# Retention's normalization in a hybrid encoder layer: squares, their sums and the gate on other buffers, the gate's silu by tanh

## The chip, the cores and the metric

The kernel runs on one core of a Trainium2 chip. A core has TensorE (matmuls; it writes to PSUM, eight banks of 128 x 512 f32), VectorE, ScalarE (functions such as exp from a table that is loaded), GpSimd, and SyncE, whose queue issues most DMAs. In the profile they are PE (with PEld for weight loads), DVE, ACT, POOL and SP. The metric is the device time of one execution in microseconds, lower is better.

## The reference

One layer on x of 1024 tokens by 1024 features, in float32:

```python
u = x @ w_in                                  # split into rq, rk, rv, rg, aq, ak, av
y_ret = retention(rq, rk, rv)                 # 8 heads of 64, both directions, chunks of 128
y_ret = groupnorm(y_ret) * gn_gain * silu(rg)
y_att = windowed_gqa(aq, ak, av, sink)        # 8 query heads, window 128, ALiBi
h = layer_norm(alpha * x + concat(y_ret, y_att) @ w_out)
f = (silu(h @ w_gate) * (h @ w_up)) @ w_down + sigmoid(h @ w_pg) * (p @ w_pe)
out = layer_norm(alpha * h + f)
```

The group norm is over the 64 values of one head and token: subtract the mean, divide by sqrt(var + 1e-5). The change concerns this norm and the factor silu(rg).

## The kernel before

**Numbers.** Large products are made of three matmuls each: every operand is split into a high part (ScalarE, L71 or L580) and the rest (VectorE, L72 or L581). The value projection is centred per head beforehand (L359 to L362), so the retention's output has mean zero and the variance is a mean of squares.

**Stages.** First the projections of the first pair of heads, then a stage that works through four pairs of heads (retention and attention), then the output projection with the first layer norm, then the feed-forward part. The change lies in the second stage; that stage and the projection behind it together are about a third of the time.

**The stage of the four pairs.** Its lines give TensorE's order by hand: a list of steps in which `F` stands for a share of the queue of projection steps (`take`, L279). A step of that queue is three matmuls of 128 x 512, eight steps make one half (512 tokens) of a projection tile, into a bank "mm"; the queue holds the values, then the keys, queries and attention queries of pairs 1 to 3, at last the gates of pairs 0 to 3 (L718). So the first three gates run beside pair 3, and the fourth in the last list (L763). ScalarE, VectorE, GpSimd and SyncE are ordered by the program's planner in this stage. Each engine executes in its order.

**PSUM.** Four names of two banks each: "mm" (projections), "s" (scores), "t" (transposes and small products) and "o" (outputs). A bank is given in turn and has to be read out before TensorE writes it again.

**Retention, for one pair and one half `hh` of 512 tokens.** `out` (Y) sums 32 small matmuls into a bank "o", squares it on ScalarE into the buffer "sq" (L480) and copies it to `y` on VectorE (L481). `norm` (M) sums the squares of each head by matmuls against a 0/1 pattern, into a bank "t" (L487); VectorE scales the sums and adds epsilon (L490), GpSimd takes the power -0.5 (L491), and ScalarE spreads the factor to 512 columns in "rb" (L493). `turn` (X) transposes the factor into a bank "t" (L498), and VectorE multiplies `y` by it and the gain (L500). Buffers "sq" and "rb" exist once.

**What else uses "sq" and "t".** `decay_k` (L375) makes the decay matrix of the next pair in "sq" (ScalarE, then GpSimd). `gate` (L696) applies silu on ScalarE to the gate's bank "mm", into "sq" (L700), and VectorE multiplies `y` by it (L701). Attention of block n: `scores` (`sco`) with an exponential on ScalarE (L533), a scaling (L539), `turn` (`trn`) which transposes the probabilities into two banks "t" that ScalarE drains (L551, L553), and `values` (`val`) into a bank "o" (L563).

**Order around the change.** In a round of pairs 1 to 3, TensorE runs M(1) of the pair before near the start, X(1) some steps later, Y(0) in the middle, then M(0), the turn of block 5, the scores of block 7, Y(1), the values of blocks 4 and 5, X(0), and the turns of blocks 6 and 7 (L758 to L761). M(1) and X(1) of the last pair are in the last list.

**Beside it**, products of the output weights and of smaller weights are split and written to DRAM for later (`put`, L579): ScalarE, VectorE and a DMA, through one or two buffers.

Of the kernel before, what the change touches and what calls it, by code (L numbers as in the profile page):

```python
# [11 lines left out]
AF = mybir.ActivationFunctionType  # L12
ALU = mybir.AluOpType
# [3 lines left out]
P = 128  # L17
# [4 lines left out]
HF = 512  # L22
# [4 lines left out]
EPS = 1e-5  # L27
# [15 lines left out]
def layer(tc, xT, xn, w_first, w_mt, w_rv, w_out, w_pg, w_pe, pT, w_gu, w_dn,  # L43
          consts, dec_b, dec_c, sink, gng, lnp, out):
    nc = tc.nc
    act, dve, pool, pe, sp = nc.scalar, nc.vector, nc.gpsimd, nc.tensor, nc.sync
# [12 lines left out]
    def nm(s):  # L59
        uid[0] += 1  # L60
        return f"{s}{uid[0]}"

    def bank(tag, shape=(P, HF)):
        tag = ROLE[tag]
        return ps.tile(list(shape), F32, tag=tag, bufs=NB[tag], name=nm("b" + tag))
# [55 lines left out]
    def a_tile(shape, name, tag=None, dt=F32):  # L121

        turnA[0] += tag is None
        return big.tile(list(shape), dt, tag=tag or f"A{turnA[0] % 2}", bufs=4, name=nm(name))
# [8 lines left out]
    def bt(shape, tag, bufs=None, dt=F32):  # L133
        return bpool.tile(list(shape), dt, tag=tag, bufs=bufs, name=nm(tag))
# [15 lines left out]
    with tc.manual_schedule(engines={mybir.EngineType.DVE, mybir.EngineType.SP}):  # L150
        for kt in range(KT):
# [4 lines left out]
            if kt == 0:  # L156
                w0 = rawt(2 * HF)
                sp.dma_start(w0[:, :HF], w_first[0][:, :HF])
                for h in range(2):
                    sl = slice(h * HF, (h + 1) * HF)  # L160
# [18 lines left out]
            for h in range(2):  # L179
                sl = slice(h * HF, (h + 1) * HF)  # L180
                split(r[:, sl], xt[:, 0, sl], xt[:, 1, sl])
            xs.append(xt)
            for m, h in ([(m, h) for m in range(4) for h in range(2)] if kt else [(m, h) for h in range(2) for m in range(4)]):
                sl = slice(h * HF, (h + 1) * HF)
# [75 lines left out]
    for h in range(2):  # L260
        sl = slice(h * HF, (h + 1) * HF)
        b = st[1, h]
# [25 lines left out]
    def mtile(idx, evac):  # L288
        hold = {}

        def load():
            hold["w"] = unit2(w_mt[idx])

        def step(h, kt):
            if kt == 0:
                hold["b"] = bank("mm")
            b, w = hold["b"], hold["w"][kt // 4]
            c = slice((kt % 4) * P, (kt % 4 + 1) * P)
            sl = slice(h * HF, (h + 1) * HF)
            mm3(b, w[:, 0, c], w[:, 1, c], xs[kt][:, 0, sl], xs[kt][:, 1, sl], kt == 0, kt == KT - 1)  # L300
            if kt == KT - 1:
                evac(b, h)

        return [load], [lambda h=h, kt=kt: step(h, kt) for h in range(2) for kt in range(KT)]

    def enqueue(tiles):

        def both(f, g):
            f()
            g()  # L310

        for f in tiles[0][0]:
            f()
        for n, (_, steps) in enumerate(tiles):
            if n + 1 < len(tiles):
                for k, f in enumerate(tiles[n + 1][0]):
                    steps[2 * k] = lambda f=f, g=steps[2 * k]: both(f, g)
            queue.extend(steps)
# [63 lines left out]
    def state_tile():  # L382
        t = bt([P, 2, NT, 64], "states")
        pool.memset(t[0:64, :, 0, :], 0.0)
        pool.memset(t[64:128, :, NT - 1, :], 0.0)
        return t

    class Retention:
# [76 lines left out]
        def out(self, hh):  # L465

            o, pt, qq = bank("o", (P, 4, P)), self.pt[hh], self.qq[hh]
            for j in range(4):
                n = 4 * hh + j
                for part in range(2):  # L470
                    for h in range(2):
                        a = slice(64 * h, 64 * h + 64)
                        v = self.i * P + 64 * h
                        if part == 0:
                            pe.matmul(o[a, j, :], rv[:, n, v:v + 64], pt[:, h, j, :], start=True, stop=False)
                        else:
                            pe.matmul(o[a, j, :], self.states[:, h, n, :], qq[:, h, j, :], start=False, stop=True)
            of = o.rearrange("p n c -> p (n c)")
            sq = self.sq = bt([P, HF], "sq", 1)
            act.activation(sq, of, AF.Square)  # L480
            dve.tensor_copy(self.half(hh), of)  # L481

        def norm(self, hh):

            b = bank("t", (P, 4, 2))
            for j in range(4):
                pe.matmul(b[:, j, :], self.sq[:, j * P:(j + 1) * P], cst[:, C_BD:C_BD + 2], start=True, stop=True)  # L487
            sm = bt([P, 3, 8], "sm", 2)
            bf = b.rearrange("p n h -> p (n h)")
            dve.tensor_scalar(sm[:, 0, :], bf, 1.0 / 64, EPS, ALU.mult, ALU.add)  # L490
            pool.tensor_tensor(sm[:, 1, :], sm[:, 0, :], cst[:, C_MH:C_MH + 1].to_broadcast([P, 8]), ALU.pow)  # L491
            r = self.r[hh] = bt([P, 4, 2, 64], "rb")
            act.activation(r.rearrange("p n h e -> p (n h) e"), sm[:, 1, :].unsqueeze(2).to_broadcast([P, 8, 64]), AF.Copy)  # L493
# [172 lines left out]
    ys = [None] * 8  # L666

    def ytile(k):
        if ys[k] is None:
            ys[k] = a_tile([P, S], "y", "A0" if k < 4 else "A1")  # L670
        return ys[k]
# [24 lines left out]
    def gate(i):  # L696
        def f(b, h):
            s = bt([P, HF], "sq", 1)
            sl = slice(h * HF, (h + 1) * HF)
            act.activation(s, b, AF.Silu)  # L700
            dve.tensor_tensor(ys[2 * i][:, sl], ys[2 * i][:, sl], s, ALU.mult)  # L701
        return mtile(10 + i, f)

    def run(steps, total):
# [11 lines left out]
    F = None  # L716
    with tc.manual_schedule(engines={mybir.EngineType.PE}):
        enqueue([mtile(0, ev_av), proj_rv(), *project(1), *project(2), *project(3), gate(0), gate(1), gate(2), gate(3)])  # L718

        spare.append(bt([P, S], "aq", 3, F32R))  # L720
        twin = lambda t: t.rearrange("p (a b) -> p a b", a=2)
        ops = [twin(spare[1]), a_tile([P, 2, HF], "pro", "A0", F32R)]
        side.extend(presplit_out(0, ops, 17.5, 4))
        side.extend(presplit_out(1, ops, 44, 4, spare[:1]))
        a = Attention(0, ytile(1))
        sco, trn, val = (lambda n: (a.scores, n)), (lambda n: (a.turn, n)), (lambda n: (a.values, n))
        run([F, F, sco(0), F, sco(1), F], 16)
        run([F, (av_turn, 0), (av_turn, 1), F, trn(0), sco(2), F, trn(1), sco(3), F, val(0), val(1), trn(2), sco(4), F,
             trn(3), sco(5), F, val(2), val(3), trn(4), sco(6), F, trn(5), sco(7), F, val(4), val(5), trn(6), (decay_q, 0),
             F, trn(7), (decay_k, 0, 0), F, val(6), val(7), (decay_k, 0, 1), F], 64)  # L730
        assert not side and not later
        y0 = ytile(0)
        side.extend(presplit_gate())
        states = state_tile()
        r = Retention(0, y0, states)
        K, M = (lambda q: (r.keys, q)), (lambda q: (r.norm, q))
        Q, X = (lambda q: (r.scores, q)), (lambda q: (r.turn, q))
        Y = lambda hh: (r.out, hh)
        run([K(0), F, K(1), F, F, (r.kv,), Q(0), F, (r.scan,), F, F, F, Y(0), Q(1),
             F, M(0), (decay_q, 1), F, (decay_k, 1, 0), Y(1), X(0), (decay_k, 1, 1), F, F], 48)  # L740
        V = []
        for i in range(1, NPAIR):
            assert i == 1 or not side, len(side)
            M1, X1 = M(1), X(1)
            r = Retention(i, ytile(2 * i), states)
            a = Attention(i, ytile(2 * i + 1))
            if i == 2:
                late = [ytile(6), ytile(7)]
                op = twin(late[1].bitcast(F32R))
                side.extend(presplit_out(2, [op], 2, 3.5, late[:1]))  # L750
                side.extend(presplit_small(0, op, 30) + presplit_small(1, op, 38))
            elif i == 3:
                op = twin(bt([P, S], "aq", 3, F32R))
                side.extend(presplit_out(3, [op], 4, 3.5, [bt([P, S], "rk", 2)]))
                side.extend(presplit_small(2, op, 32) + presplit_small(3, op, 40))
            G = [(f, i + 1, *x) for f, x in ((decay_q, ()), (decay_k, (0,)), (decay_k, (1,)))] if i + 1 < NPAIR else \
                [(lambda: None,)] * 3
            run([*V, K(0), M1, F, K(1), sco(0), F, (r.kv,), Q(0), F, sco(1), X1, F, trn(0), sco(2), (r.scan,), F, trn(1),  # L758
                 sco(3), F, val(0), val(1), F, trn(2), sco(4), F, trn(3), sco(5), F,
                 Y(0), val(2), val(3), Q(1), F, G[0], trn(4), sco(6), M(0), F, G[1], trn(5), sco(7), F,  # L760
                 G[2], Y(1), val(4), val(5), X(0), F, trn(6), F, trn(7), F], 48)  # L761
            V = [val(6), val(7)]
        run([*V, M(1), F, X(1), F, F], 16)  # L763

# [34 lines left out]
    def four(k):  # L799
        return [bank(t) for t in sets[k]]  # L800
# [143 lines left out]
    X = four("a")  # L944
# [23 lines left out]
    X = four("a")  # L968
# [121 lines left out]
    X = four("a")  # L1090
# [43 lines left out]
    Y = four("a")  # L1134
# [162 lines left out]
    n = 0  # L1297
# [425 lines left out]
```

## Time and profile before

| what | us |
|---|---|
| median of three runs | 1194.67 (1194.57 to 1194.71) |
| the profiled execution | 1191.15 |
| its span, first to last instruction | 1189.4 |

The profile is of one execution. Its mean granted TensorE clock is 0.996 of full speed. In the table of stretches, between 200 and 260 us TensorE is busy 58.12 of 60.00, between 260 and 300 it is busy 38.18 of 40.00, between 300 and 340 it is busy 38.75 of 40.00, and between 340 and 375 it is busy 32.80 of 35.00; between 375 and 480 us it waits for nothing.

How to read the rows: in a timeline, the start in us, the duration, engine, line, operation, output <- input, shapes, count, and in brackets the engine's idle time just before and what ended it. In a group of instructions, after the bar the busy time and the mean in ns of one, after the second bar the idle time before them by what ended it. In a list of waits: who waited at which line, for whom, us in total, number of times, longest.

### The profile page before, as it was taken

The page shows a single profiled execution, that of the slowest core. Times are in us where ns is not written, and L with a number is a line of the kernel's source. Part 1 is how long each engine was busy: PE and PEld are TensorE (multiplying, and loading weights), DVE is VectorE, ACT ScalarE, POOL GpSimd, SP SyncE. Part 2 cuts the span into 40 slices and gives each one's busy share as a digit, 9 for nine tenths or more (in the row PEclk, how much of TensorE's full clock was granted, in tenths as well). Part 3 has the DMA queues.
Part 4 walks back from the last instruction along what each step waited for, and adds up shares of the span by engine and source line. Part 5 has one row for each costly group of instructions (what it writes and reads, how often), then busy time and mean ns, then how long its engine had stood idle before and what let it go on. Part 6 is the DMA issues. An engine that isn't in the chain of part 4 may idle for free.

```text
span 1189.4 us, 17057 instructions
## 1 busy us (share of the span) xinstructions
PE 1172.0 (99%) x6068; PEld 971.3 (82%) x6068; DVE 759.2 (64%) x1302; ACT 546.6 (46%) x1058; POOL 366.1 (31%) x346
## 2 busy tenths in 40 slices
PE   9999999999999999999999999999999999999997
PEld 7888888887787888888888888888888888888885
DVE  4566677675647788958754555545544566774677
ACT  5666348676876257114332333233333325562463
POOL 2001011202000022003756566564756342134242
PEclk9999999999999999999999999999999999999999
DMA  6346647445346854756223321333123169999977
GB/s 250 107 154 216 239 170 245 178 146 189 106 160 224 321 216 168 276 193 207 108 102 133 134 80 63 123 133 115 63 89 133 71 203 313 361 278 211 259 174 210
DMA packets 80661, 211.71 MB, mean 178 GB/s; under 512 B 9536, under 2 KB 14784, under 8 KB 80576
## 3 DMA queue, kind: packets, MB, share of 16 engines
q1 hardware_dynamic: 71936, 193.84, 45.9%
q0 software_dynamic: 8640, 16.78, 7.9%
q8 instruction: 48, 0.79, 0.3%
q14 instruction: 37, 0.30, 0.1%
HBM read 139.29 MB, written 62.13 MB: 169 GB/s over the span
## 4 chain that ended last, share of the span: by engine, by line
PE 75%; ACT 3%; DVE 2%; issue 1%; DMA 1%; POOL 0%; DVEq 0%; ACTq 0%; POOLq 0%
PE bs L782 6%; PE bs L781 6%; PE bs L780 6%; PE bt L780 6%; PE bt L781 6%; PE bt L782 6%; PE bmm L782 5%; PE bmm L781 5%; PE bmm L780 5%; PE bo L781 5%; PE bo L782 5%; PE bo L780 5%; PE bmm L77 2%; PE bmm L79 2%; PE bmm L78 1%; PE bo L563 1%
## 5 line engine op out<-in xcount | busy, mean ns | idle before, releaser
L77 PE MATMUL bmm<-H,w 128*128 128x512 f32 x240 | 98.2, 409 | 2.0 <-ACT sq L700 2.0
L79 PE MATMUL bmm<-H,w 128*128 128x512 f32 x240 | 94.9, 395 | 0.0
L78 PE MATMUL bmm<-H,w 128*128 128x512 f32 x240 | 94.5, 394 | 0.0
L1184 POOL TENSOR_TENSOR H<-ln 128x512 f32<-128x512 f32 x22 | 28.9, 1313 | 178.4 <-DMA ln<-in_w_gu 171.8
L1214 POOL TENSOR_TENSOR ev<-ev 128x512 f32<-128x512 f32 x33 | 54.6, 1656 | 91.5 <-DVE ev L1229 40.0
L72 DVE TENSOR_TENSOR w<-H,w 128x512 fp32r<-128x512 f32 x44 | 39.9, 908 | 62.7 <-ACT w L71 62.7
L72 DVE TENSOR_TENSOR w<-raw,w 128x512 fp32r<-128x512 f32 x56 | 44.9, 810 | 49.5 <-ACT w L71 49.3
L524 POOL COPY sc<-skb 128x1 f32<-128x1 f32 x64 | 14.6, 237 | 191.2 <-PE bt L551 167.2
L1212 ACT ACTIVATE ev<-ev 128x512 f32<-128x512 f32 x33 | 20.9, 633 | 103.0 <-DVE ev L1229 103.0
L1218 POOL TENSOR_TENSOR ev<-ev,ev 128x512 f32<-128x512 f32 x44 | 62.7, 1437 | 2.6
L72 DVE TENSOR_TENSOR u<-H,u 128x512 fp32r<-128x512 f32 x47 | 37.3, 793 | 38.4 <-ACT u L71 38.1
L77 PEld LDWEIGHTS bmm<-H,w 128*128 128x128 f32 x240 | 45.5, 190 | 11.9 <-ACT sq L700 2.1
L79 PEld LDWEIGHTS bmm<-H,w 128*128 128x128 f32 x240 | 45.4, 189 | 10.1
L78 PEld LDWEIGHTS bmm<-H,w 128*128 128x128 f32 x240 | 45.6, 190 | 7.9
L71 ACT ACTIVATE u<-H 128x512 fp32r<-128x512 f32 x47 | 29.6, 631 | 43.9 <-PE bt L782 9.0
L533 ACT ACTIVATE sc<-sc,st 128x385 f32<-128x385 f32 (+1 forms) x64 | 37.2, 585 | 18.9 <-DVE st L531 18.5
L529 DVE CUSTOM_DVE_ANT_0 sc<-cst,bs,skb 128x384 f32<-128x384 f32 (+1 forms) x64 | 34.9, 576 | 13.3 <-PE bs L528 8.1
L71 ACT ACTIVATE w<-raw 128x512 fp32r<-128x512 f32 x56 | 34.4, 624 | 15.6 <-PE bo L79 8.7
L891 POOL TENSOR_TENSOR stt<-stt,cst 128x1 f32<-128x1 f32 x8 | 12.2, 1520 | 86.0 <-DVE stt L890 86.0
L1188 POOL TENSOR_TENSOR H<-raw,H 128x512 f32<-128x512 f32 x22 | 37.8, 1717 | 0.0
L71 ACT ACTIVATE w<-H 128x512 fp32r<-128x512 f32 x44 | 27.4, 622 | 21.7 <-PE bt L782 6.3
L491 POOL TENSOR_TENSOR sm<-sm,cst 128x8 f32<-128x8 f32 x8 | 14.3, 1793 | 74.4 <-DVE sm L490 68.5
(811 smaller groups left out, 3778.2 us busy)
## 6 DMA issues: line engine op xcount, KB each, us to landing
ad<-ev SPq DMA_DIRECT2D x33, 512.0 KB, 2.6
pgd<-pro SPq DMA_DIRECT2D x28, 512.0 KB, 2.9
raw<-in_w_gu SPq DMA_DIRECT2D x22, 512.0 KB, 4.4
ln<-in_w_gu SPq DMA_DIRECT2D x22, 512.0 KB, 3.5
raw<-ad SPq DMA_DIRECT2D x40, 256.0 KB, 5.9
ln<-ad SPq DMA_DIRECT2D x37, 256.0 KB, 6.3
H<-in_w_dn SPq DMA_DIRECT2D x33, 256.0 KB, 6.9
wod<-aq SPq DMA_DIRECT2D x15, 512.0 KB, 2.7
```

The costliest lines, as they stand in the source:

```text
L71: act.activation(hi, raw, AF.Copy)
L72: dve.tensor_tensor(lo, raw, hi.bitcast(F32), ALU.subtract)
L77: pe.matmul(o, lh, rh, start=start, stop=False)
L78: pe.matmul(o, lh, rl, start=False, stop=False)
L79: recent[0] = pe.matmul(o, ll, rh, start=False, stop=stop).ins.name
L533: act.activation(sc[g][:, :nk + 1], sc[g][:, :nk + 1], AF.Exp, bias=st_[:, 1, j, g:g + 1], accum_out=st_[:, 2, j, g:g + 1])
L780: pe.matmul(o, lh, rh, start=start, stop=False, skip_group_check=True)
L781: pe.matmul(o, lh, rl, start=False, stop=False, skip_group_check=True)
L782: pe.matmul(o, ll, rh, start=False, stop=stop, skip_group_check=True)
L1188: pool.tensor_tensor(s[3], a(0, 1), s[0], ALU.subtract)
L1214: pool.tensor_tensor(c[:, 1, :], c[:, 0, :], c[:, 1, :], ALU.mult)
L1218: pool.tensor_tensor(self.ev[dst][:, 0, :], left, right, op)
```

## The change

Four edits, all in the second stage. The squares go to the buffer "rb", which the factor uses too, no longer to "sq". The sums of squares are written into the first two of the 128 columns of each chunk in the output's own bank "o", which has been squared and copied by then, no longer into a bank "t"; VectorE's scaling reads them there. The gate computes silu(x) as 0.5 x (tanh(x/2) + 1), with one tanh on ScalarE and two operations on VectorE (the first reads the bank "mm"), in place of one silu and one multiplication. In TensorE's order X(0) stands ahead of Y(1), since Y(1)'s squares now overwrite what X(0) reads.

```diff
-            sq = self.sq = bt([P, HF], "sq", 1)
+            sq = self.sq = bt([P, HF], "rb")
             act.activation(sq, of, AF.Square)
             dve.tensor_copy(self.half(hh), of)
+            self.o = o
...
-            b = bank("t", (P, 4, 2))
+            b = self.o[:, :, 0:2]
             for j in range(4):
                 pe.matmul(b[:, j, :], self.sq[:, j * P:(j + 1) * P], cst[:, C_BD:C_BD + 2], start=True, stop=True)
             sm = bt([P, 3, 8], "sm", 2)
-            bf = b.rearrange("p n h -> p (n h)")
-            dve.tensor_scalar(sm[:, 0, :], bf, 1.0 / 64, EPS, ALU.mult, ALU.add)
+            dve.tensor_scalar(sm[:, 0, :].rearrange("p (n h) -> p n h", h=2), b, 1.0 / 64, EPS, ALU.mult, ALU.add)
...
             s = bt([P, HF], "sq", 1)
             sl = slice(h * HF, (h + 1) * HF)
-            act.activation(s, b, AF.Silu)
-            dve.tensor_tensor(ys[2 * i][:, sl], ys[2 * i][:, sl], s, ALU.mult)
+            act.activation(s, b, AF.Tanh, scale=0.5)
+            dve.scalar_tensor_tensor(s, s, 1.0, b, ALU.add, ALU.mult)
+            dve.scalar_tensor_tensor(ys[2 * i][:, sl], s, 0.5, ys[2 * i][:, sl], ALU.mult, ALU.mult)
...
-             F, M(0), (decay_q, 1), F, (decay_k, 1, 0), Y(1), X(0), (decay_k, 1, 1), F, F], 48)
+             F, M(0), (decay_q, 1), F, (decay_k, 1, 0), X(0), Y(1), (decay_k, 1, 1), F, F], 48)
...
-                 G[2], Y(1), val(4), val(5), X(0), F, trn(6), F, trn(7), F], 48)
+                 G[2], X(0), Y(1), val(4), val(5), F, trn(6), F, trn(7), F], 48)
```

## The prediction

> **What bounds the kernel now.** I read the page first: its span, its busy times and its chain of work.
>
> ```profile
> span 1189.4 us, 17057 instructions
> PE 1172.0 (99%) x6068; PEld 971.3 (82%) x6068; DVE 759.2 (64%) x1302; ACT 546.6 (46%) x1058; POOL 366.1 (31%) x346
> ```
>
> TensorE is busy 99% of the span, so a change to other engines is worth only what TensorE waits for them. The second view is the list of all waits of TensorE, whole:
>
> ```profile
> PE bt L487 <- ACT ptr L553: 2.9, 2, 1.8
> PE bmm L77 <- ACT sq L700: 2.0, 1, 2.0
> PE bo L142 <- POOL sq L139: 1.3, 1, 1.3
> PE bo L563 <- ACT ptr L553: 0.8, 2, 0.7
> PE bt L551 <- ACT ptr L553: 0.8, 1, 0.8
> PE bt L551 <- DVE y L500: 0.6, 1, 0.6
> ```
>
> The columns are us in total, times, longest. All of it is 8.4 us. The first two rows stand on lines that the change touches: the sums of squares (L487) wait for a bank "t" that ScalarE has not yet emptied of turned probabilities (L553), and a gate's projection (L77) waits for a bank "mm" that the silu (L700) has not yet emptied. I call the four passes over head pairs rounds 0 to 3. In the timeline the two waits of L487 are in rounds 1 and 2, before the first half's sums, M(0):
>
> ```profile
> 206.99 1.05 PE L487 MATMUL bt<-cst,sq 128*128 128x2 f32 x8 [1.09 <-ACT ptr L553]
> 270.80 1.05 PE L487 MATMUL bt<-cst,sq 128*128 128x2 f32 x8 [1.79 <-ACT ptr L553]
> ```
>
> Third, the table of stretches around the longer one (busy times of PE, PEld, DVE, ACT, POOL, then granted clock, DMA share, GB/s):
>
> ```profile
> 270.00:275.00 5.00, 4.20 (x17) 3.53 (x18) 3.02 (x10) 4.18 (x11) 2.09 (x1) 0.73 0.78 282
> 275.00:280.00 5.00, 5.00 (x42) 4.13 (x42) 1.85 (x7) 4.87 (x14) 1.90 (x4) 0.93 0.40 134
> ```
>
> The granted clock falls to 0.73 and 0.93 just behind the wait: 5 x 0.27 + 5 x 0.07 = 1.7 us of matmul time lost, which the list of waits doesn't show. A waiting TensorE pays twice there.
>
> The Trainium skill ("TensorE: Matmul & The Clock Gate", on the HAM clock gate) says that the clock halves after an idle window of about 3.4 us, and that this window runs free of the kernel. This trace differs on the length: a wait of 1.79 us was followed by the loss, while the 2.02 us wait was not. Going by the Trainium skill's length alone, the drop would not belong to this wait and the gain below would be 1.7 us smaller.
>
> **The change, part by part.**
>
> *Sums into the output's bank.* M(0) and M(1) no longer take a bank "t", so what L487 waited for is gone: 1.09 + 1.79 = 2.9 us, and with the second wait its 1.7 us of slow clock. Their new wait is for the Square and the copy that read the output's bank. Those lie well back (in the rows of the next part the Square is at 347.26, its sums at 355.72), with a share of projection between in every round. The bank "o" is held until the tensor_scalar behind the sums (L490); its next user, the values of block 4, comes only after Y(1), here at 213.37 with its 16 matmuls against
>
> ```profile
> 208.09 0.17 DVE L490 TENSOR_SCALAR sm<-bt 128x8 f32<-128x8 f32 x1 [1.07 <-PE bt L487]
> 213.10 0.84 ACT L553 ACTIVATE ptr<-bt 128x384 f32<-128x384 f32 x2
> 213.37 0.44 PE L475 MATMUL bo<-pt,rv 128*64 128x128 f32 x4
> ```
>
> so that costs nothing; without these 5 us of cover it would cost the lateness of L490.
>
> *Squares leave "sq".* A gate's silu shares the one "sq" with the Square. The wait of 2.02 us is this:
>
> ```profile
> 347.26 0.58 ACT L480 ACTIVATE sq<-bo 128x512 f32<-128x512 f32 x1
> 355.72 1.05 PE L487 MATMUL bt<-cst,sq 128*128 128x2 f32 x8
> 358.14 0.60 ACT L700 ACTIVATE sq<-bmm 128x512 f32<-128x512 f32 x1
> ```
>
> Gate 2's first half can't be drained before M(1) has read the squares of 347.26; after M(1) come a table load and the silu, while TensorE's next projection needs that bank. With the squares in "rb" the buffer is free and the drain follows its matmuls: 2.02 us gone. The DVE now releases this bank (its first new operation reads it), some 0.7 us behind the tanh; the bank is wanted again only behind the other bank's half, 24 matmuls later.
>
> *Factor turned before Y(1).* Squares and factor sharing "rb" is why X(0) moves ahead of Y(1): the Square of Y(1) has to wait for X(0)'s transposes. This is the part with a price. X(0) now comes earlier on TensorE, by Y(1) and two blocks of values, and needs two things there: the factor (L493), and a bank "t" that block 5's probabilities have left. Y(1)'s start in before is the new place of X(0):
>
> ```profile
> 155.00 0.63 ACT L493 ACTIVATE rb<-sm 128x512 f32<-128x512 f32 x1 [2.20 <-POOL sm L491]
> 155.57 0.44 PE L475 MATMUL bo<-pt,rv 128*64 128x128 f32 x4
> ...
> 274.26 0.63 ACT L493 ACTIVATE rb<-sm 128x512 f32<-128x512 f32 x1 [0.73 <-POOL sm L491]
> 276.92 0.84 ACT L553 ACTIVATE ptr<-bt 128x384 f32<-128x384 f32 x2
> 278.77 0.44 PE L475 MATMUL bo<-pt,rv 128*64 128x128 f32 x4
> ...
> 341.64 0.61 ACT L493 ACTIVATE rb<-sm 128x512 f32<-128x512 f32 x1
> 341.94 0.44 PE L475 MATMUL bo<-pt,rv 128*64 128x128 f32 x4
> 344.21 0.84 ACT L553 ACTIVATE ptr<-bt 128x384 f32<-128x384 f32 x2
> ```
>
> - Round 0: factor at 155.63, place at 155.57: 0.1 us.
> - Round 1: place 213.37 - 1.09 = 212.28. The first of the two drains of L553 ends half-way through its 0.84, at 213.5. If ScalarE stays where it is, 1.3 us; if it moves up with the sums (L490 waited 1.07 for them), 0.2. I take 0.7, the middle.
> - Round 2: place 278.77 - 1.79 - 1.7 = 275.28, first drain done at 277.35: 2.1 us. ScalarE can gain at most the 0.73 it waited before L493: 1.4. I take 1.7.
> - Round 3: place 341.94, first drain done at 344.65: 2.7 us with ScalarE as it is. But two table loads of 1.28 us go from just ahead of it (next part): 0.15. I take 0.3.
>
> Sum 2.8 us (0.5 where ScalarE's order changes in its favour in rounds 1 and 2; 6.2 at the worst). Queued behind a waiting X(0) are Y(1), values and everything after on TensorE, so all of it counts.
>
> *Tanh for silu.* The groups of rounds 3 and the end, by line:
>
> ```profile
> L700 ACT ACT_TABLE_LOAD x5 | 6.4, 1283 | 1.5 <-PE bt L487 1.4
> L533 ACT ACT_TABLE_LOAD x4 | 5.1, 1283 | 0.1
> L701 DVE TENSOR_TENSOR y<-y,sq 128x512 f32<-128x512 f32 x8 | 5.5, 691 | 6.2 <-ACT sq L700 6.2
> L500 DVE SCALAR_TENSOR_TENSOR y<-y,gn,bt 128x512 f32<-128x512 f32 x8 | 6.0, 746 | 4.4 <-PE bt L498 4.4
> ```
>
> Nine loads, 11.5 us of ScalarE, if tanh shares the exponential's table. No load of this trace shows a tanh. The Trainium skill ("ScalarE: Activation LUTs", Table sets) lists tanh in the exponential's set, and prices a switch at 2.66 us with its drain; the trace's row is 1.28. By the Trainium skill's figure X(0) in round 3 would wait for nothing, 0.3 us better than I count. On TensorE's path only this much of them shows:
>
> ```profile
> 314.08 1.28 ACT L700 ACT_TABLE_LOAD   x1
> 315.87 0.87 ACT L553 ACTIVATE ptr<-bt 128x384 f32<-128x384 f32 x2
> ...
> 336.70 1.28 ACT L700 ACT_TABLE_LOAD   x1 [0.99 <-PE bt L487]
> 338.61 1.28 ACT L533 ACT_TABLE_LOAD   x1
> ```
>
> The load at 314.08 holds the drain that the values (L563) wait 0.7 us for: 0.7 gone. The load at 356.85 is in the 2.02 already. The DVE gets two scalar_tensor_tensor of 0.75 us for one tensor_tensor of 0.69: 0.8 us more, eight times. It hides (DVE is busy 64%), except where the DVE is waited for: L551 waits 0.6 us for L500 in round 3, and a gate's multiplication runs on the DVE ahead of it. There 0.7 us more, or, if the DVE takes L500 first, 0.6 less; I take the 0.7. At the end the last gate runs beside the output projection:
>
> ```profile
> 370.30 0.39 PE L780 MATMUL bt<-w,H 128*128 128x512 f32 x1
> 371.30 0.69 DVE L701 TENSOR_TENSOR y<-y,sq 128x512 f32<-128x512 f32 x1
> 371.90 0.69 DVE L72 TENSOR_TENSOR H<-y,H 128x512 fp32r<-128x512 f32 x1
> ```
>
> The split at 371.90 is for the second product, 48 matmuls behind 370.30, so 0.8 us later costs nothing.
>
> **Sum**: 2.9 + 1.7 + 2.0 + 0.7 = 7.3 us gone, 2.8 + 0.7 = 3.5 us new, net 3.8 us. Against the profiled execution (1191.15 us; its span 1189.4) that is 1187.35; the median of the three runs shown, 1194.67, lies 3.5 us above that execution, and I carry this over: 1190.9.
>
> **Rivals.**
> - *ScalarE's order follows (full gain).* ScalarE, VectorE and GpSimd are ordered by the program's planner, which sees fewer loads and free buffers; it may drain block 5 before the decays, and X(0) then waits for nothing. For it: ScalarE loses 11.5 us of loads. Against: it is in-order behind split stores in rounds 1 and 2. All 7.3 and the remaining 0.8 of L551 gone: 1186.6.
> - *X(0) is the new wait (slower).* Round for round the upper ends, 6.2, plus 0.7, and two of these waits, in rounds 2 and 3, each bring the 1.7 us of slow clock that 1.79 us brought before: 10.3 against 7.3, +3.0: 1197.7. It decides from about 7 us of waits and slow clock before L498. For it: the place lies before the drain in rounds 1 to 3 as the rows stand. Against: the loads that delay round 3 go.
> - *The slow clock comes back* at X(0) in round 2, where I forecast 1.7 us of wait, close to the 1.79: 3.8 - 1.7 = 2.1 gained, 1192.6. Before shows both: 1.79 us was followed by the loss, 2.02 us was not.
> - *The split stores set the pace.* ScalarE stands in front of splits whose buffer a DMA still empties:
>
> ```profile
> ACT y L580 <- DMA wod<-y: 4.5, 2, 2.9
> ACT aq L580 <- DMA ped<-aq: 3.3, 2, 2.5
> ```
>
> If TensorE comes earlier, these waits grow by as much and hold later drains; the gain is given back before 370 us: 1194.7. Against: TensorE didn't wait behind the 2.5.
> - *The loads stay* (tanh not in the exponential's table): 0.7 less gained, round 3 at 2.7: 6.6 - 5.9, 1194.0.
>
> **How the numbers follow.** Forecast 0.40, full gain 0.20, slow clock back 0.10, stores 0.14, X(0) 0.12, loads stay 0.04. A measurement of this kernel tells about 0.2% (2.4 us) from no change. Faster by more: nearly all of the forecast and the full gain, little else, 0.60. Within: stores, loads, slow clock, the forecast's upper edge, 0.26. Slower: X(0) and a little of the stores, 0.14. The range reaches from the full gain, 1186.3, to half-way into the X(0) case, 1195.8.
>
> **What would show it.** Right: L487 has no wait left and writes "bo"; no table load in round 3 or behind it, up to the projection; L77 doesn't wait for the gate; clock near 1.00 at 270 to 280; L498 waits under 2 us in round 2, on ScalarE's L553. Wrong: waits at L498 or L551 that sum to over 5 us, a clock under 0.9 in another stretch, or table loads that stay.

## The result, and the profile after

| | before | after |
|---|---|---|
| median of runs side by side, us | 1194.69 (1191.71 to 1197.03, 6 runs) | 1184.63 (1183.31 to 1186.58, 6 runs) |
| the profiled execution, us | 1191.15 | 1184.56 |
| its span, us | 1189.4 | 1182.8 |

The ratio is 0.9918, with a 95% interval of 0.9901 to 0.9935: the changed kernel is 0.8% faster. The forecast of 1190.9 us had the sign and less than half of the size, and the time lies 1.7 us below the lower end of the range. The two profiled executions differ by 6.6 us, the medians by 10.1: before, the median lay 3.5 us above the profiled execution, after, it lies 0.1 above. That gap between 6.6 and 10.1 turns out to be the point of the case.

The page after, first its span and the busy times:

```profile
span 1182.8 us, 17057 instructions
PE 1169.2 (99%) x6068; PEld 969.6 (82%) x6068; DVE 765.8 (65%) x1310; ACT 534.5 (45%) x1049; POOL 366.1 (31%) x346
```

TensorE has as many instructions as before, ScalarE nine fewer (1058 to 1049), VectorE eight more. All waits of TensorE after (us in total, times, longest):

```profile
PE bt L498 <- ACT ptr L553: 1.8, 3, 1.3
PE bo L142 <- POOL sq L139: 1.3, 1, 1.3
PE bt L551 <- DVE y L500: 1.2, 1, 1.2
PE bt L781 <- ACT h0b L950: 0.3, 1, 0.3
```

4.6 us in place of 8.4. The sums of squares, the gate's projection (L77) and the values (L563) wait no more; the turn of the factor, X(0) (L498), is the new wait. The timeline of after, at the places that the prediction named:

```profile
206.59 0.95 PE L488 MATMUL bo<-cst,rb 128*128 128x2 f32 x8
213.27 0.66 PE L498 MATMUL bt<-cst,rb 128*128 128x128 f32 x4 [0.35 <-ACT ptr L553]
267.57 0.34 PE L528 MATMUL bs<-kz,aq 128*128 128x384 f32 x1
267.75 0.95 PE L488 MATMUL bo<-cst,rb 128*128 128x2 f32 x8
274.86 0.85 ACT L553 ACTIVATE ptr<-bt 128x384 f32<-128x384 f32 x2
275.38 0.66 PE L498 MATMUL bt<-cst,rb 128*128 128x128 f32 x4 [1.31 <-ACT ptr L553]
302.33 0.68 DVE L701 SCALAR_TENSOR_TENSOR sq<-sq,bmm 128x512 f32<-128x512 f32 x1
303.54 0.68 DVE L702 SCALAR_TENSOR_TENSOR y<-sq,y 128x512 f32<-128x512 f32 x1
304.21 0.73 DVE L500 SCALAR_TENSOR_TENSOR y<-y,gn,bt 128x512 f32<-128x512 f32 x1
305.00 0.44 PE L551 MATMUL bt<-cst,sc 128*128 128x128 f32 x2 [1.18 <-DVE y L500]
337.67 0.66 PE L498 MATMUL bt<-cst,rb 128*128 128x128 f32 x4 [0.15 <-ACT ptr L553]
363.24 0.39 PE L781 MATMUL bt<-w,H 128*128 128x512 f32 x1
```

The sums (now L488) read "rb", write "bo" and start without a pause: 267.57 to 267.75 is 0.18 us. In before the same step took 268.67 to 270.80, 2.13 us, of which the bracket named 1.79:

```profile
268.67 0.34 PE L528 MATMUL bs<-kz,aq 128*128 128x384 f32 x1
```

So a wait of 1.79 cost 1.95: matmuls that would have overlapped have to start afresh. X(0) waits 0.35, 1.31 and 0.15 us in rounds 1, 2 and 3. At 302.33 to 304.94 the DVE does both new products of a gate, with a split between them, and then L500, and L551 waits 1.18 for that, against 0.6 before. The output projection starts at 363.24 in place of 370.30, 7.1 us earlier; from there to the end of the span it is 819.6 us after and 819.1 before. The time came out of the second stage, nothing behind it moved. The table of stretches there (behind the bounds the length, then the busy times of PE, PEld, DVE, ACT, POOL, then granted clock, DMA share, GB/s):

```profile
270.00:275.00 5.00, 4.08 (x23) 3.15 (x21) 3.64 (x13) 5.00 (x14) 1.90 (x3) 1.00 0.85 286
275.00:280.00 5.00, 4.62 (x64) 4.15 (x65) 2.27 (x5) 4.13 (x12) 2.26 (x4) 1.00 0.28 111
```

The clock is 1.00 in both, where before had 0.73 and 0.93, though X(0)'s wait of 1.31, from 274.07 to 275.38, lies across the two. And the gate's line, between 140 and 375 us:

```profile
L700 ACT ACTIVATE sq<-bmm 128x512 f32<-128x512 f32 x8 | 4.7, 590 | 7.8 <-PE bmm L79 7.8
```

It is the tanh, and no table load is left on this line or on the exponential's (L533), which had five and four.

### The profile page after: what moved, and what is told of

Its sections match the earlier page's. It is cut to its first block, busy times and chain, and to the rows that moved or that the text cites. A ratio compares the mean times of both kernels' runs of the same rounds, so it can differ in the third digit from the quotient of the medians.

```text
span 1182.8 us, 17057 instructions
## 1 busy us (share of the span) xinstructions
PE 1169.2 (99%) x6068; PEld 969.6 (82%) x6068; DVE 765.8 (65%) x1310; ACT 534.5 (45%) x1049; POOL 366.1 (31%) x346
## 4 chain that ended last, share of the span: by engine, by line
PE 87%; ACT 5%; DVE 4%; DMA 2%; issue 1%; POOL 0%; DVEq 0%; SPq 0%; ACTq 0%; POOLq 0%
PE bs L783 6%; PE bs L781 6%; PE bs L782 6%; PE bt L781 6%; PE bt L783 6%; PE bt L782 6%; PE bmm L783 5%; PE bmm L781 5%; PE bmm L782 5%; PE bo L782 5%; PE bo L783 5%; PE bo L781 5%; PE bmm L77 4%; PE bmm L78 4%; PE bmm L79 4%; ACT sc L533 1%
## 5 line engine op out<-in xcount | busy, mean ns | idle before, releaser
L77 PE MATMUL bmm<-H,w 128*128 128x512 f32 x240 | 97.6, 407 | 0.0
L77 PEld LDWEIGHTS bmm<-H,w 128*128 128x128 f32 x240 | 45.2, 188 | 10.6 <-issue 1.2
L79 PEld LDWEIGHTS bmm<-H,w 128*128 128x128 f32 x240 | 45.2, 188 | 10.1
L533 ACT ACTIVATE sc<-sc,st 128x385 f32<-128x385 f32 (+1 forms) x64 | 37.2, 584 | 18.3 <-DVE st L531 18.0
```

What stands on the lines that cost most here:

```text
L77: pe.matmul(o, lh, rh, start=start, stop=False)
L79: recent[0] = pe.matmul(o, ll, rh, start=False, stop=stop).ins.name
L533: act.activation(sc[g][:, :nk + 1], sc[g][:, :nk + 1], AF.Exp, bias=st_[:, 1, j, g:g + 1], accum_out=st_[:, 2, j, g:g + 1])
```

## The experiments

The theory after the result: the kernel before loses time at a half-speed clock behind several of its waits, more of it in a typical run than in the one that was profiled; the change takes the waits away and so the slow clock too. The rival: the waits that were counted were too small, or an unlisted gain lies in ScalarE's and VectorE's new order.

### The kernel before again, three more profiles

An unused constant is added, which moves the line numbers by one and no instruction. The first is timed, the others are one execution each, taken later.

> The program of before, unchanged, timed with the granted clock of every run. Theory A (slow clock behind waits): before has three waits of TensorE between 1.1 and 2.0 us, and whether one is followed by a stretch of slow clock changes from run to run; then the runs differ by steps of about 1.7 us, and the slower a run, the lower its mean clock: 1.7 us is 0.0014 of mean clock, so 0.996 near 1191 us and 0.993 to 0.994 near 1196 us. Rival (the difference lies outside the core's work, or in waits): the clock is the same 0.996 in runs of 1191 and 1196 us, or the time minus the span changes by as much as the times do.

> Before once more, for one profile beside its time. Theory A: the number of slow-clock stretches behind the waits at about 206, 269 and 357 us is between 0 and 3, and the time is 1189.5 us plus 1.7 us for each. Rival: the stretches do not follow the time.

> Before, a fourth profile. Theory A: the time less what the slow clock costs between 200 and 370 us is 1188.8 to 1189.8 us, as in the three profiles so far. Rival: it lies outside by over 1.5 us.

The timed one: 1193.36 us (1191.58 to 1196.19, 12 runs), ratio 0.9995 (0.9983 to 1.0007). The time less the span is 1.7 to 1.9 us in every run, so the runs differ inside the core's work. The profiled executions took 1192.22, 1196.55 and 1196.41 us. The stretches behind M(0) in rounds 1 and 2 and behind the gate's wait, in the four profiles of before; first the one of the prediction:

```profile
205.00:215.00 10.00, 8.91 (x72) 7.49 (x72) 4.72 (x17) 8.66 (x24) 4.41 (x7) 1.00 0.70 238
270.00:280.00 10.00, 9.20 (x58) 7.66 (x60) 4.87 (x17) 9.06 (x24) 3.99 (x5) 0.83 0.59 208
358.00:368.00 10.00, 9.21 (x42) 7.64 (x43) 4.95 (x8) 5.07 (x11) 0.69 (x1) 1.00 0.42 146
```

The execution of 1192.22:

```profile
205.00:215.00 10.00, 8.87 (x45) 7.34 (x43) 4.97 (x16) 7.96 (x20) 4.59 (x7) 0.83 0.57 186
270.00:280.00 10.00, 8.09 (x37) 6.44 (x36) 5.05 (x16) 8.78 (x21) 3.99 (x5) 0.83 0.66 223
358.00:368.00 10.00, 7.98 (x38) 6.56 (x38) 4.20 (x7) 4.95 (x8) 1.64 (x1) 1.00 0.29 106
```

The one of 1196.55:

```profile
205.00:215.00 10.00, 8.83 (x45) 7.40 (x43) 5.05 (x16) 8.00 (x19) 4.45 (x6) 0.83 0.61 188
270.00:280.00 10.00, 7.73 (x30) 6.51 (x29) 3.62 (x12) 7.96 (x18) 2.91 (x4) 0.66 0.69 235
358.00:368.00 10.00, 7.97 (x49) 6.60 (x46) 2.40 (x5) 4.64 (x7) 1.63 (x1) 0.83 0.23 93
```

The one of 1196.41:

```profile
205.00:215.00 10.00, 8.56 (x41) 7.05 (x39) 4.55 (x16) 7.96 (x20) 4.14 (x7) 0.83 0.57 185
270.00:280.00 10.00, 7.68 (x37) 6.55 (x36) 5.04 (x16) 8.52 (x21) 3.76 (x5) 0.83 0.67 227
358.00:368.00 10.00, 7.97 (x27) 6.36 (x27) 2.81 (x5) 4.04 (x6) 1.63 (x1) 0.66 0.13 52
```

A clock of 0.83 over 10 us is 1.7 us lost, 0.66 is 3.4. The same program loses it at one place, at two, or at all three, once or twice over: 1.7, 3.4, 6.8 and 6.8 us. Taken off the times, what is left is 1189.4, 1188.8, 1189.7 and 1189.6 (with the losses to two digits, from stretches of 2 us: 1.72, 3.40, 6.84, 6.82). So nearly all of the 5.4 us between these executions is this clock. That one place loses twice, as at 270 us in the execution of 1196.55, was not foreseen: its expectation had at most three losses of 1.7, and there are four. The last one is the clean test, since its expectation was written as a number for the remainder: 1188.8 to 1189.8 expected, 1189.6 measured.

In steps of 2 us, the gate's wait in the execution of 1196.55:

```profile
360.00:362.00 2.00, 0.10 (x1) 0.01 (x1) 0.17 (x1) 1.81 (x3) 1.62 (x1) 0.96 0.00 0
362.00:364.00 2.00, 1.88 (x5) 1.50 (x5) 1.66 (x3) 1.60 (x4) 0.02 (x1) 0.50 0.00 0
364.00:366.00 2.00, 2.00 (x8) 1.58 (x7) 0.32 (x1) 0.00 (x0) 0.00 (x0) 0.68 0.65 262
```

TensorE rests for 1.9 us and then works for about 3.4 us at half of the clock. The list of waits has the first line of this, not the second and third.

Why the same wait is paid twice in one execution and once in another also shows in these records. A slow stretch lasts 3.41 us or twice that, and within one execution all of them start a whole number of 3.413 us apart: in that of 1196.55 at 208.25, 273.11 and 361.85 us, 19 and 26 steps. So it is in each of the 16 profiles, with the steps at another place against the kernel each time. In the profile of the prediction the wait of 1.79 us lies within one step (268.92 to 272.33), and the next step is slow; the gate's 2.02 us are parted by the edge of a step at 357.66 into 0.89 and 1.13, and no slow step follows. Over the second stage of all profiles, no step at full clock with less than 1.1 us of idle TensorE was followed by a slow one, all nine with over 1.7 us were, and of the 24 between these bounds 10 were. What decides there is open; whether the narrow matmuls beside a wait (eight of 128 x 2) count as work wasn't tested.

### The parts alone

The sums in the output's own bank, and nothing else of the change:

```diff
+            self.o = o
...
-            b = bank("t", (P, 4, 2))
+            b = self.o[:, :, 0:2]
...
-            bf = b.rearrange("p n h -> p (n h)")
-            dve.tensor_scalar(sm[:, 0, :], bf, 1.0 / 64, EPS, ALU.mult, ALU.add)
+            dve.tensor_scalar(sm[:, 0, :].rearrange("p (n h) -> p n h", h=2), b, 1.0 / 64, EPS, ALU.mult, ALU.add)
```

> Before with the sums of squares alone written into the output's bank; squares in sq, silu and the order as in before. Theory A: both waits of L487 go with the slow clock behind them, while the gate's 2.0 us stays: 4.5 us faster in the span, 5 to 7 us faster in the timed runs, mean clock 0.997 or more. Rival (ScalarE's 11.5 us of table loads carry the gain): 3 us or less, because ScalarE is as late as before and holds TensorE at the next place.

> The kernel with the bank alone changed once more, on the same chip as the filled one: median 1188.2 us. With a second profile: slow clock at 350 to 360 us or none, and the time 1186.6 us plus what is lost there.

1188.25 us (1187.09 to 1190.0), ratio 0.9953 (0.9939 to 0.9967), and again 1188.13, ratio 0.9956 (0.9943 to 0.9968). The sums' waits are gone; the list keeps the gate's:

```profile
PE bmm L77 <- ACT sq L700: 2.0, 1, 2.0
PE bt L551 <- ACT ptr L553: 1.2, 2, 0.7
```

The profiled executions had 3.4 us of slow clock behind that wait in the first and 1.7 in the second, none in rounds 1 and 2; without them 1186.6 and 1186.9 are left, where 1186.6 was expected. The gain is in the range that was foreseen, but the mean clock of 0.997 and the 4.5 us in the span weren't reached (0.996 and 1.3 us in the first), since the gate's wait brought the slow clock more often than in the profile of the prediction. This part is the largest, and it pays for the waits and for the clock behind them.

The tanh alone (the three lines of `gate`):

> Before with the gate by tanh alone. Theory A: no table load in round 3; the gate still waits for M(1) to read the squares, so of its 2.0 us only the load of 1.3 goes, and 0.7 at the values: about 2 us faster, the two waits of L487 and the slow clock stay. Rival (table loads carry the gain): 5 us or more.

1192.47 us (11 runs), ratio 0.9986 (0.9977 to 0.9994). The waits of its profile:

```profile
PE bt L487 <- ACT ptr L553: 3.5, 2, 2.1
PE bmm L77 <- DVE sq L701: 1.4, 1, 1.4
PE bt L551 <- DVE y L500: 1.2, 1, 1.2
```

The gate's wait shrinks from 2.0 to 1.4, not by the 1.3 us of the load, and doesn't go, since the squares still share "sq" with the gate there; L551 behind L500 grows from 0.6 to 1.2, as in the whole change.

The squares in "rb", with X(0) ahead of Y(1), and silu and the bank "t" as before:

```diff
-            sq = self.sq = bt([P, HF], "sq", 1)
+            sq = self.sq = bt([P, HF], "rb")
...
-                 G[2], Y(1), val(4), val(5), X(0), F, trn(6), F, trn(7), F], 48)
+                 G[2], X(0), Y(1), val(4), val(5), F, trn(6), F, trn(7), F], 48)
```

(and the same step in round 0's list.)

> Before with the squares in rb and X(0) ahead of Y(1); the sums stay in a bank t, the gate stays silu. Theory A: the gate's 2.0 us goes down to about zero, L487 waits as before, and X(0) waits up to 2.7 us in round 3 behind the table loads and 1 to 2 us in rounds 1 and 2: between 1 us faster and 3 us slower than before. Rival (sharing rb costs nothing, the order is free): 2 us faster or more.

1190.55 us (8 runs), ratio 0.9972 (0.996 to 0.9983): 0.28% faster, where the theory had it near nothing and the rival at 2 us or more. Its waits:

```profile
PE bt L487 <- ACT ptr L553: 4.1, 3, 2.2
PE bt L498 <- ACT ptr L553: 1.0, 2, 0.8
```

The gate waits for nothing here, as foreseen, and X(0) waits only 1.0. The sum of all waits hardly fell (8.4 to 7.7); most of what was gained is clock, as the table below has it. So the number is the rival's, but not its reason: the order isn't free, as the next run shows.

The order alone, X(0) ahead of Y(1), everything else as before:

> Before with X(0) ahead of Y(1) and nothing else. Theory A: the waits of L487 and the gate stay, X(0) adds 2 to 4 us of waits behind block 5's drains: 2 to 4 us slower than before, 1196 to 1199 us. Rival (ScalarE's order follows TensorE's, so that X(0) finds its bank free): within 1 us of before.

1197.84 us (12 runs), ratio 1.0023 (1.001 to 1.0036). The price of the step shows by itself:

```profile
PE bt L487 <- ACT ptr L553: 3.4, 2, 2.2
PE bt L498 <- ACT ptr L553: 2.9, 2, 2.7
```

and behind the 2.7 us, in round 3, the clock goes too (0.70 over 10 us and 0.96 over the next, 3.4 us of the 6.9 that it loses in this stage):

```profile
340.00:350.00 10.00, 7.28 (x53) 6.27 (x53) 4.31 (x12) 7.96 (x21) 0.00 (x0) 0.70 0.42 159
350.00:360.00 10.00, 10.00 (x68) 8.21 (x66) 1.98 (x3) 2.61 (x7) 0.00 (x0) 0.96 0.36 130
```

Bank, tanh, and buffer with its order, each without the others, give -0.47%, -0.14% and -0.28%, together -0.9%, and the whole change -0.82%: the parts nearly add.

### The change with one part undone

With the silu back:

> The changed kernel with the gate's silu of before (one silu, one multiplication). Theory A: the nine table loads come back; the bank and buffer parts stay. X(0) in round 3 waits up to 2.7 us instead of 0.15, the values wait 0.7 again, the wait of L551 for VectorE goes from 1.2 back to 0.6: 2 to 4 us slower than the changed kernel, 1186.5 to 1188.5 us, and where a wait of 2 us stands, slow clock in some runs. Rival (tanh's two VectorE operations cost what the loads save): within 1 us of 1184.6.

1187.76 us, ratio 0.9946 (0.9931 to 0.996), 3.1 us above the change. Its waits:

```profile
PE bt L498 <- ACT ptr L553: 3.8, 3, 1.7
PE bo L563 <- ACT ptr L553: 0.7, 1, 0.7
```

With the sums in a bank "t" again:

> The changed kernel with the sums of squares in a bank t as before; squares in rb, tanh and the order stay. Theory A: L487 waits 2.9 us or more again, with slow clock behind the longer of these waits in most runs: 4 to 7 us slower than the changed kernel, 1188.5 to 1191.5 us. Rival (with the loads gone ScalarE drains in time and the bank doesn't matter): within 1.5 us of 1184.6.

1187.84 us, ratio 0.9944 (0.9925 to 0.9962), 3.2 above the change, a little less than expected. The waits of the sums come back, and in the profile 1.7 us of slow clock at 272 us with them:

```profile
PE bt L487 <- ACT ptr L553: 3.3, 2, 2.1
```

Each of these two parts is worth some 3 us inside the whole; the buffer was not undone there. The tanh is worth 1.7 us alone and 3.1 inside, where it also keeps X(0) from waiting: 3.8 us with the silu, 1.8 with the tanh.

### Waits filled with useless matmuls

The half speed behind a wait could come from the wait, or from the place. Where matmuls fill the wait, TensorE works through it. First in before, ahead of M(0) in rounds 1 and 2, with 5 and 9 matmuls into the bank that Y(1) takes next:

```diff
+            n = {1: 5, 2: 9}.get(self.i, 0) if hh == 0 else 0
+            if n:
+                self.early = bank("o", (P, 4, P))
+                for _ in range(n):
+                    pe.matmul(self.early.rearrange("p n c -> p (n c)"), xs[0][:, 0, :P], xs[0][:, 0, :HF], start=True, stop=True)
```

> Before with 5 and 9 further matmuls of 128x512 ahead of M(0) in rounds 1 and 2, about 1.1 and 2.0 us of work whose results nobody reads: TensorE works where before it waited for the bank. Theory A (the slow clock follows the waits): TensorE arrives at M(0) when it did before or up to 0.3 us later, and the slow clock at 205 and at 270 us is gone: 2 to 3.5 us faster than before in the timed runs, 1191 to 1192.5 us. Rival (the slow clock has another cause, or it is the waits alone that cost): the same as before, or up to 1 us slower.

1194.65 us (1193.85 to 1195.68, 12 runs), ratio 1.0004 (0.9993 to 1.0015). This is what the rival had named, but the run doesn't decide: no slow clock is left behind M(0) in its profile,

```profile
205.00:215.00 10.00, 9.94 (x83) 8.28 (x83) 4.54 (x17) 8.61 (x24) 3.50 (x5) 1.00 0.61 214
270.00:280.00 10.00, 9.66 (x83) 8.07 (x83) 5.36 (x16) 8.43 (x22) 3.02 (x5) 1.00 0.68 240
```

while waits behind L500 grew from 0.6 to 2.5 (here lines behind the addition are shifted by seven), and the gate's wait, with its slow clock, stayed:

```profile
PE bt L558 <- DVE y L507: 2.5, 3, 1.3
PE bmm L77 <- ACT sq L707: 2.0, 1, 2.0
```

Its times lie closer together (1.8 us) than those of before (1190.71 to 1198.12 beside it), and its mean clock is higher, 0.9962 against 0.9940, worth 2.5 us. They were paid back elsewhere: the 3.1 us of added work took only 2.1 us out of the waits of the sums, and the waits behind L500 grew by 1.9.

The second try has one wait and no other change: the kernel with the bank part alone, and 9 matmuls (2.0 us) behind M(1) of the last pair, where the gate waits 2.0.

```diff
-        run([*V, M(1), F, X(1), F, F], 16)
+        def fill():
+            e = bank("o")
+            for _ in range(9):
+                pe.matmul(e, xs[0][:, 0, :P], xs[0][:, 0, :HF], start=True, stop=True)
+
+        run([*V, M(1), (fill,), F, X(1), F, F], 16)
```

> The kernel with the bank alone changed, and 9 further matmuls of 128x512 (2.0 us, nobody reads them) right behind M(1) of the last pair, where TensorE waits 2.0 us for the gate; that wait is the only one over 1 us that it has left. Theory A (slow clock follows waits): no slow clock at 355 us; the times lie at the low end of the bank-alone kernel's 1187.1 to 1190.0 us, median 1186.5 to 1187.3, and closer together. Rival (the slow clock has another cause): median 1188.2 us or more with the same spread, and slow clock at 355 us in the profile all the same.

1187.5 us (1186.37 to 1187.59, 5 runs), ratio 0.9949 (0.9936 to 0.9963), against 1188.13 (1187.03 to 1189.92) of the same kernel unfilled on the same chip. That is just above the theory's 1186.5 to 1187.3 and below the rival's 1188.2, and within the scatter of the unfilled kernel. Work was added and the time didn't grow; the runs lie within 1.2 us, not 2.9. The stretch unfilled:

```profile
350.00:360.00 10.00, 7.97 (x48) 6.32 (x47) 2.15 (x4) 4.63 (x7) 1.63 (x1) 0.83 0.26 106
```

and filled:

```profile
350.00:360.00 10.00, 9.74 (x53) 8.01 (x50) 3.50 (x6) 4.79 (x8) 1.63 (x1) 1.00 0.15 61
```

With the wait filled the clock stays at 1.00 in this profile. The timed runs decide, since an unfilled wait can pass too: the clock is 0.998 in all five filled runs, and 0.995 to 0.997 in the ten unfilled ones. The wait brings the slow clock, not the place.

### Where X(0) and X(1) stand

In the change, X(0) moved behind Y(1) but still ahead of the values of block 4:

```diff
-                 G[2], X(0), Y(1), val(4), val(5), F, trn(6), F, trn(7), F], 48)
+                 G[2], Y(1), X(0), val(4), val(5), F, trn(6), F, trn(7), F], 48)
```

(and in round 0 Y(1) before X(0), as it was.)

> The changed kernel with X(0) one step later: behind Y(1) and ahead of the values of block 4. Theory A: Y(1) takes about 1.8 us of TensorE, so the waits of 0.35, 1.3 and 0.15 us before X(0) are hidden, and Y(1)'s square waits only for X(0): 1.5 to 2 us faster than the changed kernel, about 1183 us. Rival (the square comes later and holds ScalarE, or the wait goes to the next transposes): no faster than 1184.6 us.

1182.79 us (1182.03 to 1183.4, 5 runs), ratio 0.9903 (0.9886 to 0.9919). L498 waits no more; one wait of the stage is left:

```profile
PE bt L551 <- DVE y L500: 1.2, 1, 1.2
```

To that, X(1) moved two steps earlier in rounds 1 to 3, so that L500 is done before L551 wants the bank:

```diff
-            run([*V, K(0), M1, F, K(1), sco(0), F, (r.kv,), Q(0), F, sco(1), X1, F, trn(0), sco(2), (r.scan,), F, trn(1),
+            run([*V, K(0), M1, F, K(1), sco(0), F, (r.kv,), Q(0), X1, F, sco(1), F, trn(0), sco(2), (r.scan,), F, trn(1),
```

> The changed kernel with X(0) behind Y(1) as in the run before, and X(1) one step list earlier, ahead of a share of projection and the scores of block 1. Theory A: the multiplication L500 then stands ahead of the gate's two operations on VectorE, and the wait of 1.2 us of L551 goes: about 1181.7 us. Rival (X(1) then waits for its factor or a bank): 1183 us or more.

1182.17 us (1181.48 to 1183.68, 5 runs), ratio 0.9898 (0.9878 to 0.9918): the fastest version of all, 2.5 us below the change, though its step over the one before (0.6 us) is within their scatter. The wait behind L500 is gone and a smaller one, behind the probabilities, shows in its place:

```profile
PE bt L551 <- ACT ptr L553: 0.6, 1, 0.6
```

### All runs by their mean clock

Each timed run has its mean granted clock over the span, to three digits, so a run's loss can be estimated as (1 - clock) x span. Means over all runs of a kernel, against all 83 runs of before (69 timed beside the experiments and 14 with the unused constant; mean 1194.17 us, clock 0.9940, loss 7.1 us). In every profile 2 to 3.5 us of the loss cost nothing: at the end of the span, behind the last matmul, the clock falls to 0.50 with no work left for TensorE. In the change's profile these are the last 4.9 us, and all of its loss. The columns of gains are differences, in which they nearly cancel; "rest" is all that the clock doesn't account for:

| kernel | mean us | clock | loss | gain: clock | gain: rest |
|---|---|---|---|---|---|
| the change | 1184.98 | 0.9977 | 2.8 | 4.4 | 4.8 |
| bank alone (both) | 1188.38 | 0.9960 | 4.8 | 2.4 | 3.4 |
| bank alone, filled | 1187.17 | 0.9980 | 2.4 | 4.7 | 2.3 |
| tanh alone | 1192.68 | 0.9942 | 6.9 | 0.2 | 1.3 |
| buffer and order alone | 1190.49 | 0.9966 | 4.0 | 3.1 | 0.6 |
| order alone | 1197.39 | 0.9928 | 8.6 | -1.5 | -1.8 |
| before, M(0)'s waits filled | 1194.62 | 0.9962 | 4.6 | 2.5 | -3.0 |
| X(0) between | 1182.74 | 0.9980 | 2.4 | 4.8 | 6.7 |

The rounding of the clock is worth up to 0.6 us in one run, about 0.1 in a mean of ten. Within before the two go together as well: the 19 runs with a clock of 0.992 or less took 1196.1 us in the mean, the 36 with 0.995 or more 1192.7. The change gains nearly as much by the clock as by all the rest; filling a wait moves gain from one column to the other, and in before so much of it that nothing was won; the buffer, which takes the 2.0 us of the gate away and pays with waits elsewhere, gains most of its 3.7 us by the clock.

## Why the prediction was right in kind and short in size

**The failed step** is this one: "the median of the three runs shown, 1194.67, lies 3.5 us above that execution, and I carry this over". The 3.5 us were no constant around the kernel. They were the slow clock behind the waits that the profiled execution happened to pass without it: M(0) in round 1, the gate, and a second helping at one place or another. The change takes these waits away, so the 3.5 us had to be on the list of what goes; after it the median lies 0.1 us above the profiled execution. That the profile shown was a quick one was chance; that the gap was taken for a constant was the error. The term beside it, 1.7 us for "its 1.7 us of slow clock" behind one wait, was the same term mis-sized: read from one execution it is 1.7, over all runs 4.4. The prediction's own rows held the hint: a 1.79 us wait with the loss, a 2.02 us wait without, and a median well above the execution.

Worked again with what the runs show: of the 9.2 us between the means of the table the clock accounts for 4.4, and 4.8 are left for the waits and the rest. The profiles give the same remainder by another way: without slow clock, before is at 1189.4 and after at 1184.56, 4.9 less. Of the 6.2 us between the forecast and the median (1190.85 and 1184.63), 3.4 are the gap carried over, 1.7 the listed waits, which fell by more than was forecast, and 1.1 are in no list.

In kind it was right: every sign that it named for that came: the sums of squares (L488 now) have no wait and write "bo", no table load is left in the stage, L77 doesn't wait for the gate, the clock is 1.00 at 270 to 280, and X(0) waits 1.31 us in round 2. Two slips in its working change nothing of this: by its own terms the low sum for X(0) is 0.4, not 0.5, and the full gain is 1186.6, where the range starts at 1186.3.

- *The sums' waits, 2.9*: right. No wait is left in any kernel with the output's bank. The bank's longer hold costs nothing, as argued: no wait for the later users of "bo" shows.
- *The gate, 2.0*: right in the whole change, and the buffer is what does it: with the tanh alone 1.4 stays, with the buffer alone nothing.
- *Values, 0.7*: right; both waits of L563 are gone with the tanh, one of 0.7 is back with the silu.
- *X(0), 2.8*: 1.8 came, 0.35 + 1.31 + 0.15 against 0.7 + 1.7 + 0.3 in rounds 1 to 3; round 0's 0.1 isn't in the list. In round 2, ScalarE started the drain that X(0) needs at 274.86 in place of 276.92, near enough to the place at 274.07. The choice between the bounds was good, one microsecond high in all.
- *L551 behind the DVE, 0.7 more*: right, 0.6 more.
- *What the forecast left to the full gain alone*: the 0.8 us of L551 behind the probabilities went too.

The listed waits fell by 3.8 us, by the prediction's own count 5.6 - 3.5 = 2.1 without the clock: the 0.8 here and 1.0 less at X(0), with 0.3 of a new wait at L781 against them, are that difference but for rounding. The 4.9 us without slow clock stand against these 3.8 of listed waits; the restart seen at 268.67 explains some of the other 1.1, and the rest isn't traced.

**The rivals.** The full gain came nearest, 1186.6, and still was 2 us short, since it carried the 3.5 as well. X(0) as the new wait is a real mechanism, +0.23% when the order is changed alone; in the whole change the loads that go and the order on ScalarE keep it small. The slow clock didn't come back at 1.31 us in the profiled execution, which by the steps counted above could have gone either way, and a mean clock of 0.9977, against 0.9980 where X(0) waits for nothing, leaves little room for it in the other runs. The loads left, as the forecast had it. The split stores took nothing back: 7.1 us gained at the first matmul of the projection are kept.

**The rule of the Trainium skill** ("TensorE: Matmul & The Clock Gate", The HAM clock gate), that the clock halves after about 3.4 us of idle time, doesn't fit the rows: rests of 1.1 to 2.7 us were followed by the loss, and filling a rest of 2.0 removed it. Its other half, a window that runs free of the kernel, fits executions of one program that differ in where they lose it, slow stretches that start whole steps of 3.413 us apart, and losses of about 1.7 us, half of such a window. By the rule's length no wait here would bring the loss, and by estimate the change would have gained 4.8 us, not 9.2.

## What to carry to other kernels

Where runs of one program spread by several microseconds and their mean clock goes with their time, the spread is a cost that a change can remove: look at more than one profiled execution before a difference between a profile and a median is carried over as a constant. On a TensorE that is otherwise busy, a wait of 1 to 2 us can cost twice its row, so taking such waits out, or shortening them, comes first; waits under 1.1 us never brought the second cost here. Covering a wait with useless matmuls kept the clock up in both tries and won no time beyond the scatter in either. And where a new wait appears because a step was moved ahead of its data, try the places in between: one step back gave 1.8 us here at no cost.

## What the runs showed of the hardware

- The granted clock of TensorE fell to 0.50 behind rests of 1.1 to 2.7 us, for 3.4 us or, at times, about twice that (1.7 or 3.4 us lost at a place). Whether it falls differs from one execution to the next: behind the same three waits of before the four profiles have 1.7, 3.4, 6.8 and 6.8 us. The changes of the clock lie on steps of 3.413 us that stand elsewhere against the kernel in each execution, and a slow step goes with the idle time in the step before it: always above 1.7 us, never below 1.1 in these profiles.
- Work put into a rest can be free where the rest would have brought the slow clock: nine more matmuls, 2.0 us, and 1187.5 us in place of 1188.1, which is no more than the scatter.
- A tanh between exponentials needs no table load; silu between exponentials needed nine, 1.28 us each. The Trainium skill ("ScalarE: Activation LUTs", Table sets) lists tanh in the exponential's set; the trace agrees.
- Sums of squares can be written into a matmul's own output bank once that has been read out: the eight small matmuls took 0.95 us there (L488), 1.05 in a bank of their own.
